# Feed-forward entry turned token-major, with modulation work redistributed between TensorE and VectorE

## The chip, the cores and the metric

The kernel runs on one core of one Trainium2 chip. The metric is the device time of one launch in microseconds (us); lower is better. The engines are named as the profile names them: PE (TensorE), DVE (VectorE), ACT (ScalarE), POOL (GpSimd) and SP (SyncE, which issues nearly all loads).

## The reference

The input is one sequence of 256 tokens with 1,024 features, all in float32. A first block (projections, an mLSTM mixer, an attention mixer, an output product, a gated unit with a norm) is followed by two layers of a second block. Cut to what matters here:

```python
c_act = silu(c)
for i in range(2):
    mod = (c_act @ mod_w[i] + mod_b[i]).reshape(B, 6, D)[:, :, None, :]
    hin = x * (1.0 + mod[:, 1]) + mod[:, 0]
    y = mla_mixer(hin, ...) if i == 0 else moba_mixer(hin, ...)
    x = layer_norm(ALPHA * x + mod[:, 2] * y, ln_g[i, 0], ln_b[i, 0])
    hin = x * (1.0 + mod[:, 4]) + mod[:, 3]
    u = hin @ ffn_w_in[i];  a, b = u[..., :D_FF], u[..., D_FF:]
    y = (gelu(causal_conv(a) + conv_b) * b) @ ffn_w_out[i]
    x = layer_norm(ALPHA * x + mod[:, 5] * y, ln_g[i, 1], ln_b[i, 1])
```

Each `mod[i][m]` is a vector of 1,024 numbers, and its weights are 4 MB, so the twelve vectors are 48 MB of loads and matrix-vector products that depend on `c` alone. They can be placed anywhere ahead of their use.

## The kernel before

**Products.** Every float32 weight tile of 128x1024 is split in two parts (`split`): ACT casts a high part `wh`, then DVE subtracts and writes a low part `wl`. Each of `wh` and `wl` has four buffers (NW), the raw loads have six of 1 MB (NR, tag "raw"). A product is three matmuls: high by high, high by low, low by high. In `mm3` the weight stands in the array and 256 tokens move (128x256); in `mm3t` a block of 128 tokens stands and 512 columns of weight move (128x512).

**Token-major stages.** `tokens` and `halves` compute a stage for token block 0 (tb 0) and then token block 1 (tb 1), both from the same split weights, in groups of weight rows k. Behind the last group of tb 0 stands `done(0)`, and behind that of tb 1 `done(1)`: `residual_moments` (DVE multiplies, adds, takes statistics), `rstd` (a power on POOL), then DVE scales the first half of x and ACT the second, and `feed` turns x by 128x128 transposes on PE (`ps_ln`) and writes its high part (`ln00h`, on ACT) and low part (`ln00l`, on DVE) for the next stage. Stages `mlay` and `mobay` (the mixers' output products) take tb 1 column by column in their last group (`by_column`), so that all four weight rows of it stay in use until the end of the stage.

**Norms.** `Norm(joint=True)` stands between a mixer and its feed-forward: it waits for both token blocks and then turns them together. Elsewhere the four pieces (first half of tb 0, then first half of tb 1, second half of tb 0, second half of tb 1) are turned one by one.

**Feed-forward entry.** The first 1,024 columns (`fi0`, `fi1`: four column blocks of the gated half and four of the other) are weight-stationary, because the norm gives x for both token blocks at once: 8 k x 8 column blocks x 3 matmuls of 128x256. Then come the other columns (`f`) and the output product (`fy`), interleaved.

**Modulation.** A vector is four units of 1 MB. A unit runs on PE (16 narrow matmuls, 8 in the order's rows, `ps_mod<-raw_mod,c`) or on DVE (two STT, short for SCALAR_TENSOR_TENSOR, of 128x1024 into `modacc`; the very first piece is an ACT multiply). `fin` closes a vector: if it has DVE parts, four more matmuls with ones sum them; then DVE adds the bias (`modr`) and PE turns the row (`modt`). `fill=N` of a stage puts N units on PE behind the last matmul of the stage, in the gap in which the norm is computed.

**What sets the order.** A scheduler with a timeline of its own orders each engine's instructions once, when the program is built; on the chip each engine takes them in that order. `issue_after` ties an instruction behind another for the scheduler, and buffers tie a split to the last use of the buffer's former content.

Of the kernel before, what the change touches and what calls it, by code (L numbers as in the profile page):

```python
# [46 lines left out]
class G:  # L47
# [182 lines left out]
    def halves(self, load, ks, x, acc, width, name, ends, done=None, fill=0, by_column=False):  # L230
# [275 lines left out]
def block1(g):  # L506
# [401 lines left out]
def gated(g, xt, hl, pw):  # L908
# [577 lines left out]
```

## Time and profile before

| | |
|---|---|
| median of 3 runs | 881.18 us (881.17 to 881.21) |
| the profiled execution | 881.07 us |
| its span, first to last instruction | 879.3 us |
| PE busy | 861.4 us, 98% |
| DVE, ACT, POOL busy | 645.9 us (73%), 482.7 us (55%), 52.9 us (6%) |
| granted clock of TensorE, mean | 0.997 |

The span is what the trace covers; about 1.8 us of the execution's time lie outside it. Times below are from the span's start. A matmul's shown duration is longer than its share of PE, since matmuls overlap: what one costs is the distance from its start to the next one's. The number in brackets behind a row is the time for which the engine sat idle before it, and what it waited for.

### The profile page before, as it was taken

To read this page: it belongs to the slowest core of one execution; us is meant where nothing else is said; L and a number is where in the kernel's file an instruction comes from. 1 tells how busy PE (TensorE), PEld (TensorE's weight loads), DVE (VectorE), ACT (ScalarE), POOL (GpSimd) and SP (SyncE) were. 2 spreads that over 40 slices of the span, in tenths; PEclk is the share of its full clock that TensorE was granted. 3 is DMA by queue.
4 is the path that set the end of the run, shared out by engine and by line. 5 is a ranking of instruction groups with operands and counts; after the bars stand their busy time and mean duration, and the time that the engine had idled before them with its cause. 6 is when DMAs were issued, how large, how long until landed. Compare 5 with 4: busy or idle time off the path is not lost. (4 is left out here: it accounts for less than half of the span.)

```text
span 879.3 us, 15479 instructions
## 1 busy us (share of the span) xinstructions
PE 861.4 (98%) x6119; PEld 776.4 (88%) x6119; DVE 645.9 (73%) x1201; ACT 482.7 (55%) x853; POOL 52.9 (6%) x81
## 2 busy tenths in 40 slices
PE   8999999999999999999999999999999999999996
PEld 7998779999888688799999899689997999999995
DVE  5798787768767585789888887575756676666676
ACT  6555666445567654476545556275553774454550
POOL 2003111000000230000000000000000000000003
PEclk9999999999999999999999999999999999999998
DMA  8955796854447972598898984598543965566311
GB/s 267 354 200 180 278 343 203 285 204 151 144 149 284 288 284 73 188 366 299 287 333 301 310 287 169 186 349 267 176 161 129 370 197 191 168 214 198 140 49 48
DMA packets 112766, 199.36 MB, mean 227 GB/s; under 512 B 8389, under 2 KB 76469, under 8 KB 112693
## 3 DMA queue, kind: packets, MB, share of 16 engines
q1 hardware_dynamic: 111892, 196.25, 65.6%
q0 software_dynamic: 496, 1.59, 0.5%
q8 instruction: 48, 0.79, 0.4%
q10 hardware_dynamic: 304, 0.53, 0.2%
q14 instruction: 26, 0.21, 0.1%
HBM read 197.28 MB, written 1.08 MB: 226 GB/s over the span
## 5 line engine op out<-in xcount | busy, mean ns | idle before, releaser
L187 PE MATMUL ps_f<-ln10h,wl_f 128*128 128x256 f32 x288 | 81.5, 283 | 0.0
L185 PE MATMUL ps_f<-ln10h,wh_f 128*128 128x256 f32 x288 | 81.5, 283 | 0.0
L186 PE MATMUL ps_f<-ln10l,wh_f 128*128 128x256 f32 x288 | 81.5, 283 | 0.0
L187 PE MATMUL ps_f<-ln00h,wl_f 128*128 128x256 f32 x288 | 81.5, 283 | 0.0
L186 PE MATMUL ps_f<-ln00l,wh_f 128*128 128x256 f32 x288 | 81.5, 283 | 0.0
L185 PE MATMUL ps_f<-ln00h,wh_f 128*128 128x256 f32 x288 | 81.4, 283 | 0.0
L172 ACT CAST wh_fo<-raw_fo 128x1024 fp32r<-128x1024 f32 x38 | 39.8, 1047 | 44.7 <-PE ps_f L186 43.5
L173 DVE TENSOR_TENSOR wl_fo<-raw_fo,wh_fo 128x1024 fp32r<-128x1024 f32 x38 | 46.5, 1223 | 20.8 <-ACT wh_fo L172 20.5
L172 ACT CAST wh_f<-raw_fa 128x1024 fp32r<-128x1024 f32 x36 | 37.5, 1048 | 39.3 <-PE ps_f L186 30.0
L974 DVE SCALAR_TENSOR_TENSOR modacc<-raw_mod,c,modacc 128x1024 f32<-128x1024 f32 x40 | 51.1, 1278 | 6.8 <-DMA raw_mod<-in_mod_w_dram 3.5
L173 DVE TENSOR_TENSOR wl_f<-raw_fb,wh_f 128x1024 fp32r<-128x1024 f32 x36 | 43.1, 1220 | 17.5 <-ACT wh_f L172 17.4
L186 PEld LDWEIGHTS ps_f<-ln00l,wh_f 128*128 128x128 f32 x288 | 55.2, 192 | 0.3
L185 PEld LDWEIGHTS ps_f<-ln00h,wh_f 128*128 128x128 f32 x288 | 55.2, 192 | 0.3
L173 DVE TENSOR_TENSOR wl_f<-raw_fa,wh_f 128x1024 fp32r<-128x1024 f32 x36 | 43.9, 1222 | 15.7 <-ACT wh_f L172 15.2
L187 PEld LDWEIGHTS ps_f<-ln00h,wl_f 128*128 128x128 f32 x288 | 55.2, 192 | 0.0
L187 PEld LDWEIGHTS ps_f<-ln10h,wl_f 128*128 128x128 f32 x288 | 55.1, 191 | 0.0
L186 PEld LDWEIGHTS ps_f<-ln10l,wh_f 128*128 128x128 f32 x288 | 55.1, 191 | 0.0
L185 PEld LDWEIGHTS ps_f<-ln10h,wh_f 128*128 128x128 f32 x288 | 55.1, 191 | 0.0
L172 ACT CAST wh_f<-raw_fb 128x1024 fp32r<-128x1024 f32 x36 | 36.6, 1047 | 29.0 <-PE ps_fy L194 22.2
L959 PE MATMUL ps_mod<-raw_mod,c 128*32 128x256 f32 x400 | 27.7, 383 | 0.9 <-DVE mod L989 0.9
L172 ACT CAST wh_fi<-raw_fi 128x1024 fp32r<-128x1024 f32 x16 | 16.9, 1074 | 14.9 <-PE ps_mlay L194 8.3
L959 PEld LDWEIGHTS ps_mod<-raw_mod,c 128*32 128x32 f32 x400 | 12.4, 109 | 11.8 <-issue 3.1
(839 smaller groups left out, 2848.1 us busy)
## 6 DMA issues: line engine op xcount, KB each, us to landing
raw_mod<-in_mod_w_dram SPq DMA_DIRECT2D x48, 1024.0 KB
raw_fo<-in_ffn_w_out_dram SPq DMA_DIRECT2D x22, 1024.0 KB
raw_fa<-in_ffn_w_in_dram SPq DMA_DIRECT2D x18, 1024.0 KB
raw_fb<-in_ffn_w_in_dram SPq DMA_DIRECT2D x18, 1024.0 KB
raw_fi<-in_ffn_w_in_dram SPq DMA_DIRECT2D x16, 512.0 KB
raw_wo<-in_w_out_dram SPq DMA_DIRECT2D x6, 1024.0 KB
raw_aqk<-in_w_in_dram SPq DMA_DIRECT2D x4, 1024.0 KB
raw_mqk<-in_w_in_dram SPq DMA_DIRECT2D x4, 1024.0 KB
```

Source lines behind the costliest of these rows:

```text
L172: self.nc.scalar.copy(hv, src)
L173: self.nc.vector.tensor_tensor(lv, src, hv.bitcast(F32), op=ALU.subtract)
L185: T.matmul(ps, wh, xh, start=start, stop=False, skip_group_check=chk)
L186: T.matmul(ps, wh, xl, start=False, stop=False, skip_group_check=chk)
L187: T.matmul(ps, wl, xh, start=False, stop=stop, skip_group_check=chk)
L959: T.matmul(st["ps"][32 * j:32 * j + 32, :], lhs, v[:, S * j:S * j + S], start=start, stop=stop, skip_group_check=True, tile_position=(0, 3 ...
L974: nc.vector.scalar_tensor_tensor(st["acc"], rv[:, e], c, st["acc"], op0=ALU.mult, op1=ALU.add)
```

## The change

The feed-forward entry becomes a token-major stage (`g.tokens` with `fload` and `fdone`): x stands, 512 weight columns move, 192 matmuls of 128x512 for each feed-forward stand where 384 of 128x256 stood. ACT copies the result to SBUF, and 16 transposes (`fit`) for each feed-forward turn it back for `gate` and `hidden`. The first two weight rows (`spare=2`) are split into raw buffers (`ws_fi`), ahead of the stage. The norm ahead of it is no longer joint; its four pieces are turned one by one, and the statistics of tb 1 are tied behind the scale of tb 0 (`g.marks`). In stages that aren't by column, the last three products (LATE) of tb 1 are tied behind the transposes of tb 0. The loads of `ukv` and `uq` stand ahead of `lat`'s modulation units, and the first two loads of `mobav` at the end of feed-forward 0.

The units on PE go from 25 to 10 and those on DVE from 23 to 38. The fills become: `pg` 2 to 0, `lat` 6 to 4, `mlay` 4 to 0, `fy0` 5 to 2, `mobay` 4 to 0. The vectors (0,4), (1,3) and (1,5) move to DVE in the stages `wo`, the moba heads and feed-forward 1, and in feed-forward 0 the slots for DVE units become two for each column block throughout. Ten vectors instead of six now have DVE parts, so 40 instead of 24 matmuls with ones close them.

```diff
@@ halves
-                ws[k] = self.split(load(k), f"{name}{k}", i >= NW)
+                ws[k] = self.split(load(k), f"{name}{k}", i < spare or i >= NW)
+        if pre is not None:
+            pre()
         self.fetch(fill)
...
-            with nullcontext() if ins is None or done is None else self.tc.issue_after(ins.ins):
-                for k, n, c in orders[tb]:
+            first = ins
+            for i, (k, n, c) in enumerate(orders[tb]):
+                with ExitStack() as ctx:
+                    if first is not None and done is not None:
+                        ctx.enter_context(self.tc.issue_after(first.ins))
+                        if self.turned is not None and not by_column and i >= len(orders[tb]) - LATE:
+                            ctx.enter_context(self.tc.issue_after(self.turned.ins))
@@ block1
-    g.tokens(a["w_out"][0], mix, [[8, 9], [10, 11], [0, 1], [2, 3], [4, 5, 6, 7]], wacc, hdone, "wo")
+    g.tokens(a["w_out"][0], mix, [[8, 9], [10, 11], [0, 1], [2, 3], [4, 5, 6, 7]], wacc, hdone, "wo",
+             each=lambda: g.bg(tensor=False))
@@ gated
-    g.tokens(a["w_ple_gate"][0], hl, [[0, 1], [2, 3, 4, 5, 6, 7]], gacc, done, "pg", fill=2)
+    g.tokens(a["w_ple_gate"][0], hl, [[0, 1], [2, 3, 4, 5, 6, 7]], gacc, done, "pg")
@@ Norm.emit
-        if self.joint:
-            todo = [((0, 1), lo + hi)] if tb else []
-        else:
-            todo = [((1,), lo), ((0,), hi), ((1,), hi)] if tb else [((0,), lo)]
+        todo = [((1,), lo), ((0,), hi), ((1,), hi)] if tb else [((0,), lo)]
@@ resid_ln
-        after = g.marks if tb and not out.joint else ()
+        after = g.marks if tb else ()
...
-        if out.joint == bool(tb):
+        if tb == 0:
             g.marks = [iv]
@@ mla
-    g.tokens(w, x, [[0, 1, 2, 3], [4, 5, 6, 7]], acc, done, "lat", width=cuts, fill=6)
+    first = []
+    g.tokens(w, x, [[0, 1, 2, 3], [4, 5, 6, 7]], acc, done, "lat", width=cuts, fill=4, pre=lambda: first.append(loads(0)))
...
-    g.tokens(a["mla_w_o_2"][0], o, [[0, 1], [2, 3], [4, 5, 6, 7]], part, lambda tb: done(tb, part), "mlay", fill=4, by_column=True)
+    g.tokens(a["mla_w_o_2"][0], o, [[0, 1], [2, 3], [4, 5, 6, 7]], part, lambda tb: done(tb, part), "mlay", by_column=True)
@@ moba
-        if (1, 3) not in g.have:
-            g.bg()
+        if st and (1, 3) not in g.have:
+            g.bg(0 if g.queue[0][1] is None else 1, tensor=False)
...
-    g.tokens(a["moba_w_o_2"][0], o, [[0, 1], [2, 3], [4, 5, 6, 7]], part, lambda tb: done(tb, part), "mobay", fill=4, by_column=True)
+    g.tokens(a["moba_w_o_2"][0], o, [[0, 1], [2, 3], [4, 5, 6, 7]], part, lambda tb: done(tb, part), "mobay", by_column=True)
@@ ffn
+    facc = g.pair(f"fi{i}")
+    ft = [g.b4(f"fi{i}t{tb}") for tb in range(2)]
...
+    def fdone(tb):
+        for n, c in enumerate(N512):
+            A.copy(ft[tb][:, c], facc(tb, n))
+
+    g.tokens(None, x, [[0, 1, 2, 3], [4, 5, 6, 7]], facc, fdone, f"fi{i}_", load=fload, spare=2)
     g.flush()
-    acc = [g.ps(f"fi{i}{n}", "A") for n in range(4)]
-    for k2 in range(0, KD, 2):
...
-                wh, wl = g.split(rv[:, j].rearrange("p e c -> p (e c)"), f"fi{i}_{k}")
-            for n in range(4):
-                for e in range(2):
-                    c = slice(512 * e + n * P, 512 * e + (n + 1) * P)
-                    g.mm3(acc[n][:, e * S:(e + 1) * S], wh[:, c], wl[:, c], *x[k], k == 0 and e == 0, k == KD - 1, chk=True)
...
     for n in range(4):
-        hidden(n, gate(n, acc[n][:, 0:S]), acc[n][:, S:2 * S])
+        ps = g.ps(f"fit{i}{n}", "A")
+        for e in range(2):
+            for tb in range(2):
+                c = 512 * e + n * P
+                T.transpose(ps[:, e * S + tb * P:e * S + (tb + 1) * P], ft[tb][:, c:c + P], g.ident)
+        hidden(n, gate(n, ps[:, 0:S]), ps[:, S:2 * S])
...
-        g.bg(2 if i == 0 and c < 16 else 1, tensor=False)
+        g.bg(1 if i else 2, tensor=False)
...
-    g.halves(load, list(range(last, NF)), hid, part, width, f"fo{i}_", ends, lambda tb: done(tb, part), 0 if i else 5, i == 1)
+    def pre():
+        if i == 0:
+            g.ahead = g.loader(a["moba_w_in_2"][0], 2048, D, "mobav")
+            g.ahead(0), g.ahead(2)
+
+    g.halves(load, list(range(last, NF)), hid, part, width, f"fo{i}_", ends, lambda tb: done(tb, part), 0 if i else 2, i == 1, pre)
```

**The entry of feed-forward 0, ACT.** `wh_fi_k` is the high part of weight row k (`ws_fi` where it is in a raw buffer), `x_72` and `x_73` are tb 0 and tb 1, `ln00h` the high part of the turned x. Behind the splits of `mlay` stood before:

```order
L172 CAST wh_fi_0_4447<-raw_fi_0_4444 128x1024
L1091 ACTIVATE x_72<-x_72,ln000nr,ln000ry 128x512
L1091 ACTIVATE x_73<-x_73,ln001nr,ln001ry 128x512
L348 ACTIVATE ln00h_4131<-ps_ln_4388,ln00ab,ln00as 128x256
L352 ACTIVATE ln00f_4393<-ps_ln_4388,ln00ab,ln00as 128x256
L348 ACTIVATE ln00h_4131<-ps_ln_4388,ln00ab,ln00as 128x256
L352 ACTIVATE ln00f_4397<-ps_ln_4388,ln00ab,ln00as 128x256
L172 CAST wh_fi_1_4475<-raw_fi_0_4444 128x1024
```

and now stands:

```order
L174 CAST wh_fi_2_4340<-raw_fi_2_4337 128x1024
L174 CAST wh_fi_3_4344<-raw_fi_2_4337 128x1024
L1104 ACTIVATE x_72<-x_72,ln000nr,ln000ry 128x512
L174 CAST wh_fi_4_4489<-raw_fi_4_4486 128x1024
L174 CAST wh_fi_5_4493<-raw_fi_4_4486 128x1024
L361 ACTIVATE ln00h_4112<-ps_ln_4269,ln00ab,ln00as 128x128
L365 ACTIVATE ln00f_4274<-ps_ln_4269,ln00ab,ln00as 128x128
L361 ACTIVATE ln00h_4112<-ps_ln_4269,ln00ab,ln00as 128x128 x2
```

Four casts of weight rows 2 to 5, two on either side of the scale of `x_72`, now stand ahead of the first piece of `ln00h`, where one cast stood. The order of feed-forward 1 reads the same with `fi1`, `ln10` and `mobay` for `fi0`, `ln00` and `mlay`.

**The same place on DVE.** `ln00nr`, `ln00t` and `ln00st` are steps of the norm, `wl_fi_k` the low part of weight row k, `ln00l` the low part of the turned x. From the scale of `x_72` on, before:

```order
L1089 SCALAR_TENSOR_TENSOR ln000nr<-ln000mv,ln000ry 128x1
L1090 TENSOR_SCALAR x_72<-x_72,ln000mv,ln000ry 128x512
L1061 SCALAR_TENSOR_TENSOR x_73<-x_73,ln001t_4375 128x256
L1062 BN_STATS ln001st<-x_73 128x6
L1063 BN_AGGR ln001mv<-ln001st 128x2
L1069 TENSOR_SCALAR ln001v<-ln001mv 128x1
L1089 SCALAR_TENSOR_TENSOR ln001nr<-ln001mv,ln001ry 128x1
L1090 TENSOR_SCALAR x_73<-x_73,ln001mv,ln001ry 128x512
L173 TENSOR_TENSOR wl_fi_0_4448<-raw_fi_0_4444,wh_fi_0_4447 128x1024
L984 SCALAR_TENSOR_TENSOR modr_4861<-ps_mod_4332,modb_4862 128x256
L353 TENSOR_TENSOR ln00l_4133<-ln00f_4393,ln00h_4131 128x256
```

and now:

```order
L1103 TENSOR_SCALAR x_72<-x_72,ln000mv,ln000ry 128x512
L175 TENSOR_TENSOR ws_fi_1_4334<-raw_fi_0_4328,ws_fi_1_4334 128x1024
L1073 TENSOR_TENSOR ln001t_4376<-ps_mlay_4145,row_ln00m 128x512
L1073 TENSOR_TENSOR ln001t_4380<-ps_mlay_4152,row_ln00m 128x256
L1073 TENSOR_TENSOR ln001t_4384<-ps_mlay_4159,row_ln00m 128x256
L175 TENSOR_TENSOR wl_fi_2_4341<-raw_fi_2_4337,wh_fi_2_4340 128x1024
L175 TENSOR_TENSOR wl_fi_3_4345<-raw_fi_2_4337,wh_fi_3_4344 128x1024
L1074 SCALAR_TENSOR_TENSOR x_73<-x_73,ln001t_4376 128x512
L1074 SCALAR_TENSOR_TENSOR x_73<-x_73,ln001t_4380 128x256
L1074 SCALAR_TENSOR_TENSOR x_73<-x_73,ln001t_4384 128x256
L175 TENSOR_TENSOR wl_fi_4_4490<-raw_fi_4_4486,wh_fi_4_4489 128x1024
L175 TENSOR_TENSOR wl_fi_5_4494<-raw_fi_4_4486,wh_fi_5_4493 128x1024
```

The first `ln00l` now stands behind one split into a raw buffer, the six steps of tb 1's statistics that carry `x_73`, and four more splits. On PE the units of `mod` that stood behind the last matmul of `mlay` are gone: four transposes of `x_72` and the product of `ws_fi_0` with `ln00h` follow directly.

**The stretch ahead of `wo` on DVE.** `mz`, `pw` and `wo` are weight products of the first block, `mzt`, `mnum` and `mixl` steps of its gate; `modacc` is vector (0,4). From the split of `wl_mz5` on, before:

```order
L173 TENSOR_TENSOR wl_mz_0_2520<-raw_mz_2480,wh_mz_0_2519 128x1024
L865 SCALAR_TENSOR_TENSOR mzt_2399<-mzt_2399,ps_mz_2370 128x256
L179 TENSOR_TENSOR mixl_2330<-mzt_2363,mixh_2328 128x256
L866 SCALAR_TENSOR_TENSOR mzt_2399<-to_2050,mzt_2399 128x256
L867 TENSOR_TENSOR mzt_2399<-mzt_2399,mnum_1825 128x256
L173 TENSOR_TENSOR wl_mz_0_2558<-raw_mz_2554,wh_mz_0_2557 128x1024
L865 SCALAR_TENSOR_TENSOR mzt_2437<-mzt_2437,ps_mz_2408 128x256
L179 TENSOR_TENSOR mixl_2330<-mzt_2399,mixh_2328 128x256
L866 SCALAR_TENSOR_TENSOR mzt_2437<-to_2108,mzt_2437 128x256
L867 TENSOR_TENSOR mzt_2437<-mzt_2437,mnum_1907 128x256
L173 TENSOR_TENSOR wl_mz_0_2594<-raw_mz_2554,wh_mz_0_2593 128x1024
```

and now:

```order
L175 TENSOR_TENSOR wl_mz_0_2520<-raw_mz_2480,wh_mz_0_2519 128x1024
L878 SCALAR_TENSOR_TENSOR mzt_2399<-mzt_2399,ps_mz_2370 128x256
L181 TENSOR_TENSOR mixl_2330<-mzt_2363,mixh_2328 128x256
L879 SCALAR_TENSOR_TENSOR mzt_2399<-to_2050,mzt_2399 128x256
L990 SCALAR_TENSOR_TENSOR modacc_2791<-raw_mod_2828,c,modacc_2791 128x1024
L880 TENSOR_TENSOR mzt_2399<-mzt_2399,mnum_1825 128x256
L175 TENSOR_TENSOR wl_mz_0_2558<-raw_mz_2554,wh_mz_0_2557 128x1024
L878 SCALAR_TENSOR_TENSOR mzt_2437<-mzt_2437,ps_mz_2408 128x256
L990 SCALAR_TENSOR_TENSOR modacc_2791<-raw_mod_2828,c,modacc_2791 128x1024
L181 TENSOR_TENSOR mixl_2330<-mzt_2399,mixh_2328 128x256
L175 TENSOR_TENSOR wl_mz_0_2594<-raw_mz_2554,wh_mz_0_2593 128x1024
L879 SCALAR_TENSOR_TENSOR mzt_2437<-to_2108,mzt_2437 128x256
```

Two of the seven STT of the vector stand in these rows; four more stand between here and the split of `wl_wo_10`, and one stands two splits earlier.

## Rows read from the trace of the kernel before

**Rows 1.** The page, part 1: busy time of each engine.

```profile
PE 861.4 (98%) x6119; PEld 776.4 (88%) x6119; DVE 645.9 (73%) x1201; ACT 482.7 (55%) x853; POOL 52.9 (6%) x81
```

**Rows 2.** The page, part 5: one STT of a modulation unit.

```profile
L974 DVE SCALAR_TENSOR_TENSOR modacc<-raw_mod,c,modacc 128x1024 f32<-128x1024 f32 x40 | 51.1, 1278 | 6.8 <-DMA raw_mod<-in_mod_w_dram 3.5
```

**Rows 3.** Windows: busy us of PE, PEld, DVE, ACT, POOL; PEclk; DMA.

```profile
185.00:225.00 40.00, 40.00 (x270) 36.92 (x269) 32.80 (x64) 24.11 (x41) 0.00 (x0) 1.00 0.47 156
...
396.00:560.00 164.00, 164.00 (x1145) 151.85 (x1145) 135.39 (x187) 84.84 (x123) 0.55 (x1) 1.00 0.78 272
```

**Rows 4.** Timeline of PE: `mlay`, modulation, `ln00`, `fi0`, first `f` product.

```profile
360.08 0.39 PE L192 MATMUL ps_mlay<-wh_mlay,mlaoh 128*128 128x512 f32 x1
360.31 0.39 PE L193 MATMUL ps_mlay<-wl_mlay,mlaoh 128*128 128x512 f32 x1
...
365.76 3.66 PE L959 MATMUL ps_mod<-raw_mod,c 128*32 128x256 f32 x64
369.35 0.55 PE L343 MATMUL ps_ln<-ident,x 128*128 128x128 f32 x3
...
371.44 0.74 PE L185 MATMUL ps_fi<-ln00h,wh_fi 128*128 128x256 f32 x4
...
395.45 0.28 PE L185 MATMUL ps_f<-ln00h,wh_f 128*128 128x256 f32 x1
```

**Rows 5.** Timeline of ACT in the same place.

```profile
364.79 1.05 ACT L172 CAST wh_fi<-raw_fi 128x1024 fp32r<-128x1024 f32 x1 [8.31 <-PE ps_mlay L194]
367.21 0.81 ACT L1091 ACTIVATE x<-x,ln000nr,ln000ry 128x512 f32<-128x512 f32 x1 [1.36 <-DVE ln000nr L1089]
```

**Rows 6.** Timeline of DVE and POOL in the same place.

```profile
354.81 3.49 DVE L173 TENSOR_TENSOR wl_mlay<-raw_mlay,wh_mlay 128x1024 fp32r<-128x1024 f32 x3
...
359.83 1.29 DVE L1060 TENSOR_TENSOR ln000t<-ps_mlay,row_ln00m 128x512 f32<-128x512 f32 x2 [1.53 <-PE ps_mlay L194]
...
362.24 1.28 DVE L1062 BATCH_NORM_STATS2 ln000st<-x 128x6 f32<-128x512 f32 x2
...
365.60 0.67 POOL L303 TENSOR_TENSOR ln000ry<-ln000v,mhalf 128x1 f32<-128x1 f32 x1 [33.33 <-DVE ln000v L1069]
```

**Rows 7.** Timeline of ACT and DVE behind `fy0`: feed pieces of 128x128.

```profile
564.12 0.46 ACT L348 ACTIVATE ln01h<-ps_ln,ln01ab,ln01as 128x128 fp32r<-128x128 f32 x1 [4.17 <-PE ps_ln L343]
564.48 0.45 ACT L352 ACTIVATE ln01f<-ps_ln,ln01ab,ln01as 128x128 f32<-128x128 f32 x1
...
566.25 0.41 DVE L350 TENSOR_SCALAR ln01f<-ps_ln,ln01as,ln01ab 128x128 f32<-128x128 f32 x1
```

**Rows 8.** Timeline of PE: `mobay` to first `f` product of FFN 1.

```profile
676.74 3.66 PE L959 MATMUL ps_mod<-raw_mod,c 128*32 128x256 f32 x64
...
706.47 0.28 PE L185 MATMUL ps_f<-ln10h,wh_f 128*128 128x256 f32 x1
```

**Rows 9.** Timeline of DVE and PE: `fy0` to `mobaq`.

```profile
559.02 0.54 DVE L1090 TENSOR_SCALAR x<-x,ln010mv,ln010ry 128x512 f32<-128x512 f32 x1
...
562.44 1.06 PE L959 MATMUL ps_mod<-raw_mod,c 128*32 128x256 f32 x12
...
594.32 0.28 PE L185 MATMUL ps_mobaq<-ln01h,wh_mobaq 128*128 128x256 f32 x1
```

**Rows 10.** Timeline of PE: `pg` to `kn`.

```profile
270.01 0.63 PE L959 MATMUL ps_mod<-raw_mod,c 128*32 128x256 f32 x6
...
302.45 0.39 PE L185 MATMUL ps_kn<-ckh,wh_ukv 128*128 128x256 f32 x1
```

**Rows 11.** Timeline of DVE and PE: first split of `wo`, and its use.

```profile
205.94 1.23 DVE L173 TENSOR_TENSOR wl_wo<-raw_wo,wh_wo 128x1024 fp32r<-128x1024 f32 x1 [0.19 <-ACT wh_wo L172]
...
208.78 0.40 PE L193 MATMUL ps_wo<-wl_wo,ha0h 128*128 128x512 f32 x1
```

**Rows 12.** Timeline of PE in FFN 0: the products that end one modulation vector.

```profile
429.48 0.64 PE L959 MATMUL ps_mod<-modacc,ones 128*32 128x256 f32 x8
```

**Rows 13.** Windows at the end of the program (columns as in rows 3).

```profile
876.00:879.30 3.30, 0.00 (x0) 0.00 (x0) 0.11 (x1) 0.00 (x0) 0.00 (x0) 0.50 0.45 159
```

More of the change, by code (lines that the diff above doesn't have):

```diff
@@ L33 @@
 WARM = 15
+LATE = 3
 NW, NR = 4, 6
@@ L65, in __init__ @@
         self.queue, self.early, self.have = [], [], set()
+        self.ahead = None
     def ps(self, name, tag):
@@ L261, in halves, with tokens @@
             self.pending = lambda: done(1)
-    def tokens(self, w, x, groups, acc, done, name, c0=0, width=None, fill=0, by_column=False):
+    def tokens(self, w, x, groups, acc, done, name, c0=0, width=None, fill=0, by_column=False, pre=None, load=None, spare=0, each=None):
         width = (N512, TAIL) if by_column else (width or N512,) * 2
-        load = self.loader(w, c0, width[0][-1].stop, name)
+        load = load or self.loader(w, c0, width[0][-1].stop, name)
         for ks in groups:
-            end = (done, fill, by_column) if ks is groups[-1] else ()
+            end = (done, fill, by_column, pre) if ks is groups[-1] else (None, 0, False, None, spare)
             self.halves(load, ks, x, acc, width, name, (groups[0][0], groups[-1][-1]), *end)
+            spare = 0
+            if each is not None and ks is not groups[-1]:
+                each()
     def loader(self, w, c0, n, name):
@@ L1083, in done @@
         z, h = prev[tb], f"{name}{tb}"
-        cols = TAIL if tb and out.joint else N512
-        after = g.marks if tb and not out.joint else ()
+        cols = TAIL if tb and j == 0 else N512
+        after = g.marks if tb else ()
         mean, var = residual_moments(g, h, z, lambda n: acc(tb, n), cols, scale, after)
@@ L1197, in done, with loads @@
         A.copy(kx[:, t], p2[:, 0:P])
+    def loads(hf):
+        rv = g.wload(a["mla_w_ukv_2"][0], 0, 2, 1024 * hf, 1024, f"ukv{hf}")
+        raw = g.raw(f"uq{hf}")[:, 0:2 * 768].rearrange("p (k c) -> p k c", k=2)
+        for k in range(2):
+            src = a["mla_w_uq_2"][0][k * P:(k + 1) * P, 768 * hf:768 * hf + 768].rearrange("p (h c) -> p h c", h=4)
+            nc.sync.dma_start(raw[:, k, 0:512].rearrange("p (h c) -> p h c", h=4), src[:, :, 0:P])
+            nc.sync.dma_start(raw[:, k, 512:768].rearrange("p (h c) -> p h c", h=4), src[:, :, P:192])
+        return rv, raw
     acc = lambda tb, n: lacc(tb, n, (256, 320)[n])
[L1200 removed]
+    first = []
+    g.tokens(w, x, [[0, 1, 2, 3], [4, 5, 6, 7]], acc, done, "lat", width=cuts, fill=4, pre=lambda: first.append(loads(0)))
     g.flush()
@@ L1224, in units @@
     def units(hf):
-        rv = g.wload(a["mla_w_ukv_2"][0], 0, 2, 1024 * hf, 1024, f"ukv{hf}")
-        raw = g.raw(f"uq{hf}")[:, 0:2 * 768].rearrange("p (k c) -> p k c", k=2)
-        for k in range(2):
-            src = a["mla_w_uq_2"][0][k * P:(k + 1) * P, 768 * hf:768 * hf + 768].rearrange("p (h c) -> p h c", h=4)
-            nc.sync.dma_start(raw[:, k, 0:512].rearrange("p (h c) -> p h c", h=4), src[:, :, 0:P])
-            nc.sync.dma_start(raw[:, k, 512:768].rearrange("p (h c) -> p h c", h=4), src[:, :, P:192])
+        rv, raw = first.pop() if first else loads(hf)
         with ExitStack() as ctx:
@@ L1304, in moba @@
     vacc = g.pair("mobav")
+    load = g.ahead or g.loader(w, 2048, D, "mobav")
     vt = [g.b4(f"mobav{tb}") for tb in range(2)]
```

46 lines of the change are left out of this document (22 added, 24 removed).

## The prediction

> **What bounds the kernel now.** I read the page's busy times first: PE is busy for 861.4 of 879.3 us, 98% [rows 1]. So the kernel is a single line of PE work, and the time can change in two ways only: PE gets less to do, or it waits more. Next come the windows, which tell where another engine is near its own limit and could make PE wait: DVE is busy for 32.80 of 40 us ahead of and in `wo`, and for 135.39 of 164 us in feed-forward 0 [rows 3]. Last come the timelines at each place where a norm stands between two stages, since there PE has nothing of its own to do and lives on modulation units: behind `mlay` the 64 instructions of four units fill the time from 365.76 to 369.35 us, that is 0.90 us for a unit, and the first product of `fi0` follows at 371.44 us [rows 4]. The question is what PE does in these gaps when the units are gone.
>
> **The plain sum of PE work.** Start-to-start prices: 0.23 us for a 128x512 product (360.08 to 360.31) and 0.12 us for a 128x256 one: `fi0` with its 192 products takes 24.0 us, from 371.44 to 395.45, waits included [rows 4]. The 15 units that leave PE are worth 15 x 0.90 = 13.5 us. The 384 entry products of 0.12 us become 192 of 0.227 us: -2.5 us. The 32 transposes back cost about 0.11 us each, as the twelve of the norm between 369.35 and 371.44 do without their wait: +3.5 us. Four more vectors have to be closed by ones-products, which take 0.64 us a time where one can see them in feed-forward 0 [rows 12]: +2.6 us. If PE never waited for more than before, the sum would be -13.5 - 2.5 + 3.5 + 2.6 = -9.9 us. The units do not vanish, though: they become 26 more STT of 1.28 us on DVE [rows 2]. So I work through the gaps one by one.
>
> **The two feed-forward entries.** This is the step that decides. Let E = 365.76 us be the end of `mlay`. Tb 0 is finished early enough: its chain starts on DVE at 359.83, each pair of steps takes 1.2 us, and the statistics are through by 363.5 [rows 6]; with about 0.4 us for the two small steps, 0.67 us on POOL and 0.7 us for `nr` and the scale, the first half of x is scaled at 365.4. PE can therefore turn it at E, in four transposes, to 366.2.
> Then the built order bites. ACT: the first cast of a weight row of the entry waits for `mlay` and started at 364.79 before, since only then a buffer comes free [rows 5]; nothing in the change frees it earlier. In the new order two casts of 1.05 us, the scale of x (0.81 us, of which 0.75 until the next can start) and two more casts all stand ahead of the first `ln00h`: 364.79 + 4 x 1.05 + 0.75 = 369.7, and the piece itself takes 0.36 us until the next one starts [rows 7], so PE gets it at 370.0. DVE: from 365.4 on, one split (three took 3.49 us, so 1.16 each [rows 6]), three products of the statistics (0.65 + 0.35 + 0.35), two splits, three additions (1.35), two splits: 365.4 + 5 x 1.16 + 2 x 1.35 = 373.9, and `ln00l` is there at 374.1. PE waits from 366.2 to 370.0, does the four products that need only the high part, to 370.9, and waits again to 374.1. The other 20 products of tb 0 take 4.54 us and wait some 0.4 us for the next low parts, which now share DVE with tb 1's statistics: 379.0. By then tb 1 is scaled. Twelve transposes (1.3) to 380.3, 72 products (16.3) to 396.6, 16 transposes back (1.75): the columns `f` start, in effect, at 398.4, where they started at 395.45 [rows 4]. So a saving of four units (3.6 us) turns into a **loss of 2.9 us**. At the entry of feed-forward 1 the same instructions stand in the same order, and the stretch before is as long (676.74 to 706.47, 29.73 us, against 29.69 [rows 8]): another **2.9 us**. Bounds for each: at best PE waits only for ACT and DVE to do the feed of tb 0 at once, which would give -2 us; at worst the waits are 1 us longer: +4 us.
>
> A pause of PE can cost twice. At the end of the program, with no matmul left, the granted clock is 0.50 in the last 3.3 us [rows 13], which is the lower of the two levels, 1.2 of 2.4 GHz; everywhere else in the rows it is 1.00. The two pauses of an entry, 3.8 and 3.2 us with 0.9 us of products between, are longer than any in the trace before the end. If the clock fell there and the 24 products of tb 0 ran at half speed, an entry would lose 5.4 us more. The Trainium skill states the rule in "TensorE: Matmul & The Clock Gate", section "HAM oscillation — how this bites in real kernels": leave no long idle gaps on PE, or it is throttled again and starts cold. By that rule the sum below would rise by up to 10.8 us; the trace agrees only in so far as the clock does fall when PE has run out of work. I keep it as a rival.
>
> **The gap behind `fy0`.** Here x of tb 0 is scaled at 559.6 and `fy0` ends at 562.44 [rows 9], so the new early transposes and the first loads of `mobav` work: one split now precedes the scale (1.2 us, so 560.8), the transposes stand ahead of the last nine products, and the first `ln01h` is ready when the two remaining units end (564.3). Ones-products (0.65), 24 products of tb 0 (5.45) to 570.4; tb 1's statistics, between the feeds on DVE, are through at about 571.8; twelve transposes (1.3), 72 products (16.3), some 0.7 us of small waits: `mobaq` starts at 590.1 where it started at 594.32. **Gain 4.2 us** (2 to 4.5).
>
> **Between `pg` and `kn`.** Before, 270.01 to 302.45 [rows 10]. Four units go (3.6 us); of the first two about 1.2 us comes back as a wait for tb 1's scale, since the 24 products of `lat` for tb 0 last 3.1 us only; one `modt` moves away and the casts of `ukv` come earlier. **Gain 2.9 us** (1 to 3.6).
>
> **The stretch ahead of `wo`.** Vector (0,4) puts seven STT here. DVE is idle for 7.2 of 40 us [rows 3] and gets 7 x 1.2 = 8.4 us, so it must fall behind by 1.2 us at least. `wl_wo8` was written from 205.94 to 207.17 and first used at 208.78 [rows 11]: 1.6 us of slack. Going along the order with 1.2 us for each STT, I find that split at 208.3 to 209.5 and the next one about 1.1 us late too. **Loss 1.5 us** (0 to 4: the unit's loads wait for buffers that late splits release).
>
> **Closing the vectors.** The four more groups of ones-products stand inside dense PE work: **loss 2.6 us** (2 to 3.5).
>
> **At nothing.** The other STT: in feed-forward 0 five more, 6 us on a DVE that is busy for 135 of 164 us [rows 3], so 86% instead of 82%; without that cover each would cost 1.2 us. Those among the moba heads and in feed-forward 1 fall where DVE is less busy still. The copies of `fi` on ACT stand beside products.
>
> **Sum.** 2.9 + 2.9 - 4.2 - 2.9 + 1.5 + 2.6 = +2.8 us on the profiled execution of 881.07 us, which lies 0.11 us under the median: 884.0 us.
>
> **The rivals.**
> 1. *The entries gain.* Place: ACT and DVE at E. If the four casts could run before `mlay` ends, or the feed got ahead of them, each entry would give -2 instead of +2.9 us, and the sum becomes 2.8 - 9.8 = -7.0: 874 us. It decides when `ln00l` is there by about 371 instead of 374. For it: PE has x at 366.2. Against it: the order of both engines, and the buffers released at 364.79 only.
> 2. *PE work alone counts.* No gap opens anywhere: -9.9, 871 us. For it: PE at 98%. The Trainium skill's "Perfetto Trace Analysis", section "Identifying the Most-Contended Engine", says to optimise the engine with the highest occupancy first, which the change does. Against it: the gaps above.
> 3. *The clock falls* in the entries: +5 to +10 us, 889 to 895. For it: two pauses of over 3 us almost next to each other. Against it: 0.9 us of products stand between, and no such pause stands in the trace before the end.
> 4. *The change does nothing measurable*: the entries lose a little less and `wo` nothing, and it all cancels. Within 0.2% (1.8 us), which is about what a measurement of this kernel can tell from no change.
>
> **How the numbers follow.** Entries lose, sum as above, 880.5 to 888: 0.57, of which 0.10 falls within 0.2%. Rival 1: 0.22. Rival 2: 0.07. Rival 3: 0.10. The rest, 0.04, ends within 0.2% by other ways. So faster 0.29, same 0.14, slower 0.57. The predicted time is that of the likeliest case, 884.0 us; its own range is 880.5 to 888. For 8 in 10 the range has to take in rival 1 and the near end of rival 3: 873 to 889.
>
> **What would show it.** Right: in the timeline of PE behind `mlay` and `mobay`, two waits of 3 to 4 us, the first ended by ACT's `ln00h`, the second by DVE's `ln00l`; `f` begins 32 to 33 us after the end of `mlay` instead of 29.7; `mobaq` about 27.7 us after the end of `fy0` instead of 31.9; DVE over 36 of 40 us ahead of `wo`. Wrong: `ln00l` within 5 us of the end of `mlay`, or a granted clock under 1.00 there. The prediction fails most easily on the entries, which carry 5.8 us of loss where 7 us were saved.

## The result and the profile after

| | before | after |
|---|---|---|
| median | 881.17 us | 902.81 us (901.79, 902.81 and 903.94) |
| ratio | | 1.0245, 95% interval 1.0228 to 1.0262 |
| the profiled execution, and its span | 881.07, 879.3 us | 901.79, 900.0 us |
| granted clock of TensorE, mean | 0.997 | 0.984 |

The change costs 21.6 us; forecast were 2.8. One execution of the changed kernel (1059.25 us, clock 0.748) and one of `e_old_warm` (3984.96 us) were disturbed, and the medians and ratios leave them out.

The page of after, part 1, which answers to [rows 1]:

```profile
PE 861.7 (96%) x5751; PEld 767.8 (85%) x5751; DVE 680.7 (76%) x1259; ACT 493.7 (55%) x881; POOL 52.2 (6%) x81
```

PE is busy for as long as before, though 15 units left it, and idle for 38.3 us instead of 17.9. Windows of after (columns as in [rows 3]):

```profile
185.00:225.00 40.00, 38.29 (x264) 34.28 (x263) 35.25 (x62) 21.08 (x36) 0.00 (x0) 1.00 0.69 242
...
372.00:380.00 8.00, 6.17 (x15) 4.39 (x14) 6.57 (x18) 2.01 (x5) 0.60 (x1) 0.50 0.86 274
380.00:384.00 4.00, 4.00 (x24) 3.42 (x24) 1.44 (x2) 2.15 (x4) 0.00 (x0) 0.95 0.01 4
...
396.00:560.00 164.00, 161.75 (x1138) 149.03 (x1139) 138.03 (x187) 90.59 (x130) 0.00 (x0) 0.99 0.79 275
...
408.00:416.00 8.00, 7.94 (x67) 7.73 (x65) 8.00 (x13) 5.08 (x9) 0.00 (x0) 1.00 0.67 238
416.00:420.00 4.00, 1.82 (x4) 1.49 (x5) 4.00 (x8) 3.83 (x10) 0.00 (x0) 0.74 0.82 284
420.00:424.00 4.00, 4.00 (x21) 2.60 (x20) 4.00 (x10) 0.45 (x2) 0.00 (x0) 0.83 0.64 208
...
691.00:701.00 10.00, 7.27 (x16) 5.28 (x17) 8.06 (x19) 3.45 (x9) 0.55 (x1) 0.50 0.87 280
...
730.00:738.00 8.00, 5.72 (x43) 5.34 (x43) 8.00 (x16) 5.87 (x11) 0.00 (x0) 1.00 0.72 229
```

Two things stand out: a granted clock of 0.50 in both entries (372 to 380 and 691 to 701 us), and a DVE without a free moment from 408 to 424 us and from 730 to 738 us, where PE waits. The timeline of PE in after, which answers to [rows 4, 9, 10]:

```profile
273.79 0.28 PE L194 MATMUL ps_lat<-wh_lat,fnh 128*128 128x256 f32 x1
...
303.64 0.28 PE L187 MATMUL ps_kn<-ckh,wh_ukv 128*128 128x256 f32 x1
...
367.28 0.60 PE L356 MATMUL ps_ln<-ident,x 128*128 128x128 f32 x4
371.41 0.80 PE L194 MATMUL ps_fi<-ws_fi,ln00h 128*128 128x512 f32 x1 [3.52 <-ACT ln00h L361]
372.00 0.63 PE L195 MATMUL ps_fi<-ws_fi,ln00h 128*128 128x512 f32 x1
372.43 0.63 PE L194 MATMUL ps_fi<-ws_fi,ln00h 128*128 128x512 f32 x1
...
375.31 1.22 PE L196 MATMUL ps_fi<-ws_fi,ln00l 128*128 128x512 f32 x2 [1.83 <-DVE ln00l L366]
...
382.37 1.47 PE L356 MATMUL ps_ln<-ident,x 128*128 128x128 f32 x12
...
390.83 1.21 PE L196 MATMUL ps_fi<-wh_fi,ln00l 128*128 128x512 f32 x4 [1.06 <-DVE ln00l L366]
...
402.65 0.36 PE L187 MATMUL ps_f<-ln00h,wh_f 128*128 128x256 f32 x1
...
405.73 1.69 PE L1417 MATMUL ps_fit<-ident,fi0t 128*128 128x128 f32 x14
...
418.18 0.80 PE L194 MATMUL ps_fy<-wh_fo,fh0h 128*128 128x512 f32 x1 [2.25 <-ACT fh0h L180]
...
577.55 1.93 PE L975 MATMUL ps_mod<-raw_mod,c 128*32 128x256 f32 x32
...
603.71 0.28 PE L187 MATMUL ps_mobaq<-ln01h,wh_mobaq 128*128 128x256 f32 x1
...
691.69 0.79 PE L194 MATMUL ps_fi<-ws_fi,ln10h 128*128 128x512 f32 x1 [3.52 <-ACT ln10h L361]
...
695.80 1.22 PE L196 MATMUL ps_fi<-ws_fi,ln10l 128*128 128x512 f32 x2 [2.04 <-DVE ln10l L366]
...
736.57 0.50 PE L194 MATMUL ps_fy<-wh_fo,fh1h 128*128 128x512 f32 x1 [2.28 <-ACT fh1h L180]
...
739.52 0.50 PE L196 MATMUL ps_fy<-wh_fo,fh1l 128*128 128x512 f32 x1 [0.83 <-DVE fh1l L181]
```

Both pauses are there in each entry, ended by the engines that were forecast. But the products between and behind them start 0.43 us apart (372.00, 372.43) where a product of this size takes 0.23 us in [rows 4]: half the pace. And two waits follow that were not forecast, at 390.83 and 418.18 us; in feed-forward 1 there are two as well, at 736.57 and 739.52 us. The timeline of DVE shows what DVE did ahead of them (`wl_wo` answers to [rows 11]; `fs` are steps of the gate of the first hidden columns):

```profile
208.38 1.22 DVE L175 TENSOR_TENSOR wl_wo<-raw_wo,wh_wo 128x1024 fp32r<-128x1024 f32 x1
...
372.70 2.35 DVE L175 TENSOR_TENSOR wl_fi<-raw_fi,wh_fi 128x1024 fp32r<-128x1024 f32 x2
374.97 0.28 DVE L366 TENSOR_TENSOR ln00l<-ln00f,ln00h 128x128 fp32r<-128x128 f32 x1
...
389.29 1.28 DVE L990 SCALAR_TENSOR_TENSOR modacc<-raw_mod,c,modacc 128x1024 f32<-128x1024 f32 x1 [2.94 <-DMA raw_mod<-in_mod_w_dram]
390.49 0.49 DVE L366 TENSOR_TENSOR ln00l<-ln00f,ln00h 128x128 fp32r<-128x128 f32 x2
...
414.96 1.27 DVE L990 SCALAR_TENSOR_TENSOR modacc<-raw_mod,c,modacc 128x1024 f32<-128x1024 f32 x1
416.15 1.21 DVE L175 TENSOR_TENSOR wl_fo<-raw_fo,wh_fo 128x1024 fp32r<-128x1024 f32 x1
417.29 1.40 DVE L1387 TENSOR_TENSOR fs<-fs,ps_fit 128x256 f32<-128x256 f32 x4
```

At 389.29 us DVE has waited 2.94 us for the load of a modulation unit, and the `ln00l` that PE needs stands behind it. At 414.96 us an STT and a split stand ahead of the step that `fh0h` waits for. ACT begins the gate of the first hidden columns late, too. Before, the timeline of ACT has it at

```profile
393.60 1.17 ACT L1360 ACTIVATE fs<-ps_fi,cols 128x256 f32<-128x256 f32 x2
```

and in after at

```profile
406.64 1.93 ACT L1380 ACTIVATE fs<-ps_fit,cols 128x256 f32<-128x256 f32 x4
```

Where the time went, from the starts of the same products in the two traces (the terms of the forecast beside them; the closing of vectors, +2.6, was not put at a place):

| stretch | forecast | measured |
|---|---|---|
| start to end of `mlay` | +1.5 - 2.9 | +1.6 |
| end of `mlay` to first `fy0` | +2.9 | +9.6 |
| rest of feed-forward 0 | 0 | +3.9 |
| `fy0` to `mobaq` | -4.2 | -5.7 |
| `mobaq` to end of `mobay` | 0 | +1.5 |
| end of `mobay` to first `fy1` | +2.9 | +7.7 |
| rest of feed-forward 1 | 0 | +2.1 |

### The profile page after: what moved, and what is told of

The parts are those of the page before. It is cut to its first block, busy times and chain, and to the rows that moved or that the text cites. A ratio compares the mean times of both kernels' runs of the same rounds, so it can differ in the third digit from the quotient of the medians.

```text
span 900.0 us, 14848 instructions
## 1 busy us (share of the span) xinstructions
PE 861.7 (96%) x5751; PEld 767.8 (85%) x5751; DVE 680.7 (76%) x1259; ACT 493.7 (55%) x881; POOL 52.2 (6%) x81
## 5 line engine op out<-in xcount | busy, mean ns | idle before, releaser
L990 DVE SCALAR_TENSOR_TENSOR modacc<-raw_mod,c,modacc 128x1024 f32<-128x1024 f32 x66 | 84.4, 1279 | 30.2 <-DMA raw_mod<-in_mod_w_dram 18.2
L174 ACT CAST wh_f<-raw_fb 128x1024 fp32r<-128x1024 f32 x36 | 36.7, 1047 | 26.2 <-PE ps_fy L196 19.9
L1383 ACT ACTIVATE fs<-fs 128x256 f32<-128x256 f32 x44 | 17.8, 413 | 8.9 <-DVE fs L1382 8.7
L174 ACT CAST wh_fi<-raw_fi 128x1024 fp32r<-128x1024 f32 x12 | 12.1, 1044 | 17.4 <-PE ps_mlay L196 8.3
L1380 ACT ACTIVATE fs<-ps_f,cols 128x256 f32<-128x256 f32 x36 | 19.9, 554 | 0.0
```

Source lines behind the costliest of these rows:

```text
L174: self.nc.scalar.copy(hv, src)
L990: nc.vector.scalar_tensor_tensor(st["acc"], rv[:, e], c, st["acc"], op0=ALU.mult, op1=ALU.add)
L1380: A.activation(s, pa, AF.Identity, bias=cb[:, n:n + 1], scale=cw[:, 2, n:n + 1])
L1383: A.activation(s, s, AF.Gelu_apprx_tanh)
```

## The experiments

All times are medians, ratios are to the kernel before. "Fills" are the four units behind each of `mlay` and `mobay` that the change removed. A new edit makes the scheduler move other instructions as well: in e_warm and e_old_warm, for example, some splits and STT stand in another order on DVE from the second half of the entry on.

**Idle transposes in the first pause** (e_warm). After, with 34 transposes that nothing reads behind the first four of each entry.

```diff
+    wps = g.ps(f"warm{i}", "V")
+    with g.tc.issue_after(g.tail.ins):
+        for _ in range(34):
+            T.transpose(wps[:, 0:P], g.ident, g.ident)
```

> The changed kernel with 34 idle 128x128 transposes (about 3.7 us at full clock) behind the first four transposes of each feed-forward entry, which compute nothing that is used; no wait of the real work is taken away. If the lost time is mostly the halved clock: the granted clock stays at 1.00 in at least the first pause, the entry products cost 0.23 us instead of 0.43 us, and the time falls by 5 to 9 us to 893 to 897. If it is the waits and the order themselves, the clock matters little: within 2 us of the changed kernel's 902.8.

899.38 us, 1.0205 (1.0188 to 1.0223): 3.4 us less than after, between its two forecasts. The first pause is filled, the second stays, as the timeline of PE shows,

```profile
375.62 1.22 PE L196 MATMUL ps_fi<-ws_fi,ln00l 128*128 128x512 f32 x2 [2.71 <-DVE ln00l L367]
```

and the granted clock still falls: 0.87 in 360 to 380 us (after: 0.75) and 0.91 in 680 to 700 us (after: 0.78). So this run doesn't give the price of the clock.

**Feed first** (e_feed). The splits of weight rows 2 to 5 are tied behind the feed of tb 0.

```diff
+    lead = {2: g.fed[1], 3: g.fed[3], 4: g.fed[3], 5: g.fed[3]}
+    g.tokens(..., spare=2, lead=lead)
```

> The changed kernel with the splits of entry rows 2 to 5 tied behind the feed pieces of token block 0, nothing else. If the order of splits and feed makes the two pauses (and these the fall of the clock): first product within 2 us of the end of the mixer's output product, no second pause over 1 us, clock 1.00, and the time falls by 9 to 14 us to 889 to 894. If the entry's late result and the later stages cost the time whatever happens in the gap: it falls by less than 4 us.

897.80 us, 1.019 (1.0175 to 1.0206). No pause in the entries is longer than 1.8 us now, and the clock is 1.00 in 360 to 380 and 680 to 700 us. Yet only 5.0 us return, between the two forecasts, because the waits for the low parts and the hidden columns stay, as the timeline of PE in this kernel shows:

```profile
416.10 0.50 PE L194 MATMUL ps_fy<-wh_fo,fh0h 128*128 128x512 f32 x1 [2.00 <-ACT fh0h L180]
...
420.60 0.47 PE L194 MATMUL ps_fy<-wh_fo,fh0h 128*128 128x512 f32 x1 [0.87 <-DVE fs L1389]
```

A full clock in the entries was not enough.

**Fills back** (e_fill), and **the entry of before without fills** (e_oldentry): the change's two main parts, each undone alone.

```diff
-... part, lambda tb: done(tb, part), "mlay", by_column=True)
+... part, lambda tb: done(tb, part), "mlay", fill=4, by_column=True)
```

(and the same for `mobay`), and for e_oldentry the `ffn` entry, `joint` and `resid_ln` as they stood before. In e_fill vector (1,5), now on PE, is also summed in the buffer that it had before.

> The changed kernel with the four modulation units back on TensorE behind each mixer's output product (eight units, so vectors (0,5) and (1,5) on TensorE). If the pauses and the clock are the loss: units fill the first pause, the clock stays at 1.00, VectorE has 14 fewer long instructions in the feed-forwards, and the time falls by 10 to 16 us to 887 to 893. If the token-major entry costs the time itself: it falls by less than 5 us, since 7.2 us of unit work comes back onto TensorE.

> The changed kernel with the old feed-forward entry (weight-stationary, both token blocks turned together) and everything else as changed, so also without units behind the mixers' output products. If the new entry is the loss: 875 to 882, since the gap behind the first feed-forward and the stretch ahead of the latent stage gave 8 us and the ones-products and the stretch ahead of the output product of block 1 took 5 us. If the missing units are the loss (pause, then a halved clock): TensorE stands idle for 4 us at each entry, the clock falls there, and the time is 885 to 895.

e_fill: 884.12 us, 1.0029 (1.0019 to 1.0039). e_oldentry: 884.67 us, 1.0038 (1.0023 to 1.0053). Each alone takes away most of the 21.6 us: 18.7 us by the one, 18.1 by the other. e_fill is below its forecast, e_oldentry between its two. The loss is made by the two together.

**Both undone** (e_old_fill), and **the new entry alone in the kernel before** (e_newentry; the diff is the `ffn` entry of the change, with `spare`, `load` and the norms that go with it). Its counterpart **fills and feed first** (e_fill_feed) joins the edits of e_fill and e_feed.

> The changed kernel with the old entry and with four units back behind each mixer's output product; what is left of the change is vector (0,4) in the stretch ahead of the output product of block 1, the empty gap behind the gated stage, the earlier loads, the late products, vector (1,3) on VectorE and two units instead of five behind feed-forward 0. If these parts are worth what the timelines showed (1.2 to 1.9 us lost before the first mixer's end, 5.7 us won behind feed-forward 0, about 1 us for each further closing of a vector): 876 to 880, faster than before. If the won time is given back later: 881 or more.

> The kernel before with the token-major entry and the norm half by half ahead of it, and no other part of the change: all 25 units stay on TensorE, four of them in each gap. If the entry costs little while its gap is filled and VectorE is not loaded: 881 to 885, for 1 us more TensorE work and 1 to 2 us of waits at each entry. If the entry is slow in itself (copies, transposes back, late hidden columns): 888 or more.

> The changed kernel with four units back behind each mixer's output product and with the splits of entry rows 2 to 5 tied behind the feed of token block 0. Against the kernel with the units alone (882.6 to 885.4): if the remaining pauses of 1.6 us and 2.5 us in its entries come from splits ahead of the feed, it is 2 to 4 us faster, 879 to 882. If they come from VectorE being full whatever the order: within 1 us of it.

e_old_fill: 878.85 us, 0.9967 (0.9956 to 0.9978), faster than both kernels by little, as forecast. e_newentry: 886.29 us, 1.0053 (1.0037 to 1.0069), between its two forecasts. e_fill_feed: 883.03 us, 1.0013 (1.0003 to 1.0024), 1.1 us from e_fill, so the order of the splits matters little once the units are back. So the rest of the change is worth about -2.5 us, and the token-major entry costs about 5 us even with its gaps filled:

| | entry of before | token-major entry |
|---|---|---|
| with fills | 878.85 | 884.12 |
| without fills | 884.67 | 902.81 |

Without the entry the missing fills cost 5.8 us, with it 18.7: 12.9 us belong to neither alone.

**Units out of the heads** (e_late). No DVE unit in the first two column blocks of each feed-forward, three for each block later in feed-forward 0.

```diff
-        g.bg(1 if i else 2, tensor=False)
+        g.bg(0 if c < 8 else 1 if i else 3, tensor=False)
```

> The changed kernel with no modulation unit on VectorE in the first two column blocks of each feed-forward (three units a block later in feed-forward 0), nothing else. If the output product's wait on the first hidden columns comes from the long modulation instructions that share VectorE with the gate: the waits of 2.4 us (feed-forward 0) and 3.5 us (feed-forward 1) ahead of and in the first output products fall under 0.7 us, the wait for a low part inside the entry (1.2 us) goes, and the time falls by 5 to 9 us to 894 to 898. If that wait comes from the transposes back alone: less than 2 us.

900.85 us, 1.0209 (1.0192 to 1.0226): 2 us less than after. The wait ahead of `fy0` is gone, but the gain is lost again: two of the waits that came instead, late in feed-forward 0, in the timeline of PE:

```profile
528.62 0.38 PE L187 MATMUL ps_f<-ln00h,wh_f 128*128 128x256 f32 x1 [1.31 <-ACT wh_f L174]
...
563.51 0.80 PE L195 MATMUL ps_fy<-wl_fo,fo_16h 128*128 128x512 f32 x1 [2.08 <-DVE wl_fo L175]
```

So the units cost time in both places that were tried in this stage, and the next runs change their number. This run also speaks against a rival, that the STT cost time only because DVE stands still for their loads: it waits 18.2 us in all for such loads in after and 2.4 us here, and the time falls by 2 us only.

**Fewer units on DVE** (e_drop), and **that with feed first** (e_feed_drop). The DVE additions of vectors (0,5) and (1,5) are left out, so these two vectors are incomplete; loads and products stay.

```diff
-                    else:
+                    elif m != 5:
                         nc.vector.scalar_tensor_tensor(st["acc"], rv[:, e], c, st["acc"], op0=ALU.mult, op1=ALU.add)
```

> The changed kernel with the six VectorE additions of two modulation vectors, (0,5) and (1,5), left out in the column heads and entries (their values stay incomplete; all loads and products remain). Theory A (VectorE's added scalar-tensor-tensor units delay the low parts and the late hidden columns): the first fy product no longer waits, and the time falls by 8 to 10 us to about 893. Theory B (order of the splits and the clock alone): it falls by 2 us or less, 899 to 903.

> The same two vectors' additions left out, and the splits of later pieces tied behind the feed of the first. Theory A+B (split order and VectorE's load are together all of the entries' loss): 884 to 888. If a third cause is at work (the transposes moved back, the products' own pace), it stays above 890.

The expectation counts six additions; the edit takes out 14 STT, seven for each vector. e_drop: 891.89 us, 1.0125 (1.0107 to 1.0143). e_feed_drop: 884.62 us, 1.0044 (1.0027 to 1.0061). The first is a little beyond the forecast of theory A, the second within its own. In e_drop, 52 STT of units instead of 66, the first `fy0` product follows the last `f` product at once, though the pauses of the entries are those of after (3.52 and 1.82 us in feed-forward 0) and the clock is low there too (0.84 and 0.74 in its windows 360 to 380 and 680 to 700 us, 0.75 and 0.78 in after); the timeline of PE:

```profile
417.25 0.28 PE L189 MATMUL ps_f<-ln00h,wl_f 128*128 128x256 f32 x1
417.37 0.40 PE L194 MATMUL ps_fy<-wh_fo,fh0h 128*128 128x512 f32 x1
```

In e_feed_drop the pauses are short too, and the products run at 0.23 us, in the timeline of PE:

```profile
368.08 0.50 PE L194 MATMUL ps_fi<-ws_fi,ln00h 128*128 128x512 f32 x1 [0.55 <-ACT ln00h L363]
368.42 0.39 PE L195 MATMUL ps_fi<-ws_fi,ln00h 128*128 128x512 f32 x1
368.65 0.39 PE L194 MATMUL ps_fi<-ws_fi,ln00h 128*128 128x512 f32 x1
```

| | splits first | feed first |
|---|---|---|
| 66 STT | 902.81 | 897.80 |
| 52 STT | 891.89 | 884.62 |

10.9 us for 14 STT, 7.3 us more for the order with the clock: 18.2 of the 21.6 us. e_fill has 52 STT as well, with eight more units on PE, which by [rows 4] are 7.2 us of work; it takes as long as e_feed_drop. So the work that the change took from PE in these gaps had cost next to nothing.

**The clock alone** (e_old_warm). e_oldentry with 34 idle transposes behind `mlay` and `mobay`.

```diff
+        if by_column and name != "fo1_":
+            wps = self.ps(f"warm{name}", "V")
+            with self.tc.issue_after(ins.ins):
+                for _ in range(34):
+                    self.nc.tensor.transpose(wps[:, 0:P], self.ident, self.ident)
```

> The entry of before in the changed kernel's other parts, without the four fill units behind mlay and mobay, and 34 idle transposes (nothing reads them) in their place. Theory 'clock': the 6 us between this kernel without and with the fill units are the price of TensorE's clock, so 877.5 to 879.5 us. Theory 'load': they are the price of the units that VectorE then carries, so 882 us or more.

880.76 us, 0.9999 (0.9989 to 1.0009), between the two forecasts: of the 5.8 us that part e_oldentry from e_old_fill the idle transposes give back 3.9, and 1.9 stay. The timelines of PE behind `mlay`, first of e_oldentry:

```profile
369.04 0.63 PE L356 MATMUL ps_ln<-ident,x 128*128 128x128 f32 x3 [1.94 <-DVE x L1106]
371.49 2.18 PE L356 MATMUL ps_ln<-ident,x 128*128 128x128 f32 x9 [1.82 <-DVE x L1106]
373.32 1.20 PE L187 MATMUL ps_fi<-ln00h,wh_fi 128*128 128x256 f32 x4
...
374.53 0.41 PE L189 MATMUL ps_fi<-ln00h,wl_fi 128*128 128x256 f32 x1
374.75 0.41 PE L187 MATMUL ps_fi<-ln00h,wh_fi 128*128 128x256 f32 x1
```

and of e_old_warm:

```profile
366.87 3.87 PE L274 MATMUL ps_warmmlay<-ident 128*128 128x128 f32 x34
...
371.43 1.20 PE L361 MATMUL ps_ln<-ident,x 128*128 128x128 f32 x9 [0.36 <-DVE x L1111]
372.63 0.74 PE L187 MATMUL ps_fi<-ln00h,wh_fi 128*128 128x256 f32 x4
...
373.77 0.28 PE L189 MATMUL ps_fi<-ln00h,wl_fi 128*128 128x256 f32 x1
373.89 0.28 PE L187 MATMUL ps_fi<-ln00h,wh_fi 128*128 128x256 f32 x1
```

The last nine transposes begin at about the same moment in both (371.49 and 371.43 us), but a 128x256 product costs 0.22 us in the one and 0.12 in the other, at a granted clock of 0.83 and of 1.00 in 360 to 380 us. Up to these rows nothing differs but the idle transposes and the clock. From the last product of the mixer to the first of `fy0` and `fy1` the two kernels are 1.75 and 1.54 us apart: 3.3 of the 3.9 us. The rest lies later in feed-forward 0, where the order differs too.

**The `wo` stretch relieved** (e_best3). e_old_fill without units tied to the splits of `wo`, with two fills behind `pg`, and one vector's rest on DVE in the mla heads.

```diff
-    g.tokens(..., wacc, hdone, "wo",
-             each=lambda: g.bg(tensor=False))
+    g.tokens(..., wacc, hdone, "wo")
...
-... gacc, done, "pg")
+... gacc, done, "pg", fill=2)
...
-            g.bg(0 if g.queue[0][1] is None else 1)
+            g.bg(0 if g.queue[0][1] is None else 1, tensor=False)
```

> The entry of before, the fill units back at mlay and mobay, no units tied to each split in the wo stretch, two fill units back ahead of pg, one vector's rest on VectorE in the mla heads. If the 2.2 to 2.7 us by which pg starts late come from VectorE's units in the wo stretch, 875 to 877.5; if not, 878 to 880.

880.08 us, 0.999 (0.9981 to 1.0), 1.2 us above e_old_fill and at the upper end of the second forecast. `pg` starts at 247.49 us, as before (247.54), instead of 249.76 in e_old_fill, so the loss ahead of `pg` does come from the units in `wo`. The time does not follow, since DVE is late one stage further on, in the timeline of PE:

```profile
294.46 0.44 PE L1002 MATMUL ps_modt<-ident,modr 128*128 128x128 f32 x2 [3.09 <-DVE modr L999]
298.23 1.34 PE L1206 MATMUL ps_ltT<-ident,lt 128*128 128x128 f32 x4 [3.33 <-DVE lt L1197]
```

## Why the prediction was wrong in size

The direction was right, and so was the cause that was given for it, the pauses of the entries. Two steps failed: the pace of PE behind the pauses, and the cover of the STT.

**Right: what ends the pauses, and when.** PE was to get `ln00h` 4.2 us and `ln00l` 8.3 us after the end of `mlay`; it got them at 371.41 and 375.31, 4.1 and 8.0 us after 367.28, ended by ACT and DVE as said. Rival 1 is excluded. The second pause is 1.83 us and not 3.2, mostly because the four products ahead of it ran at half pace.

**Wrong: "the other 20 products of tb 0 take 4.54 us".** From 375.31 to 382.37 they took 7.06 us, most of it at the lower level of the clock (0.50 until 380 us, 1.2 GHz). At 0.23 us each they would have taken 4.6 us, so the clock cost 2.5 us in this entry, and 2.6 us in feed-forward 1 (695.80 to 703.02 us), where the window has the same 0.50. The four products between the pauses were slow as well, but that only shortened the wait for `ln00l`. This is rival 3, which I had priced at 5.4 us an entry, given a chance of 0.10 and left out of the sum; a granted clock under 1.00 in the entries stood among the signs of being wrong. The argument against it, that 0.9 us of products stand between the pauses, did not hold. The columns `f` begin 35.4 us behind the end of `mlay` (402.65 - 367.28), not 32 to 33. (In each feed-forward 96 products of 128x512 stand where 192 of 128x256 stood; 192 and 384 are the two together.) The Trainium skill ("TensorE: Matmul & The Clock Gate", section "HAM oscillation — how this bites in real kernels") warns of just such idle gaps; the trace agrees, with the 0.50 above. By that rule alone the sum would have been 2.8 + 10.8 = 13.6 us, and 894.7 us, so it too leaves 7 us unexplained.

**Wrong: "At nothing: the other STT".** The cover was read from a mean over 164 us. That mean came out as forecast (138.03 of 164 us by the window of after, 84% against 86%), but in the head of the stage DVE has no free moment (408 to 424 us), and what PE waits for stands in DVE's order behind STT and splits. Before, the gate's first step on ACT stood at 393.60 us, ahead of the first `f` product at 395.45; now the columns are copied and turned back first (405.73 us), and that step stands at 406.64, 4 us behind the first `f` product. So what stands between the gate's steps on DVE is on the path: 2.25 us of waits in feed-forward 0, 2.28 and 0.83 in feed-forward 1, behind STT and splits together. The 1.06 us in the entry are the STT that waited for its load; in feed-forward 1 an STT at 726.89 us, ahead of the gate's steps, held DVE for 2.76 us in the same way. e_drop puts 10.9 us on the 14 STT. Its trace shows where: against after, the way from the end of `mlay` to the first `fy0` is 3.4 us shorter, the rest of feed-forward 0 3.1, the way from the end of `mobay` to the first `fy1` 2.3 and the rest of feed-forward 1 1.2. From `mobaq` to the end of `mobay` it is as long as after, so the +1.5 us there do not come from these STT.

**Undersized: the stretch ahead of `wo`.** `wl_wo8` was forecast at 208.3 to 209.5 us and stands at 208.38 to 209.60. But `pg` starts 3.4 us late, not 1.5 and a group of closing matmuls: PE waits 1.7 us (44.29 of 46 us busy from 205 to 251 us), and the rest, in which the closing of (0,4) lies, was not taken apart. DVE was to be over 36 of 40 us busy and was at 35.25.

**Right: `pg` to `kn`.** From the end of `pg` to `kn` it takes 303.64 - 273.79 = 29.9 us against 32.4 in [rows 10]: 2.6 us gained, forecast 2.9.

**Right, and better: behind `fy0`.** 603.71 - 577.55 = 26.2 us against 31.9 in [rows 9]: 5.7 us gained, forecast 4.2. In e_old_fill this stretch is as short, and it is the only one in which that kernel is clearly ahead of the kernel before. Three units fewer on PE, at 0.90 us by [rows 4], make 2.7 us of it; the rest is left to the early transposes and loads, which no run undid alone.

**How it adds up.** From the last product of the mixer to the first product of `fy0` or `fy1`, in us, by the starts in the traces:

| | to `fy0` | to `fy1` |
|---|---|---|
| before | 41.41 | 41.46 |
| new entry alone (e_newentry) | 43.97 | 43.88 |
| after | 51.02 | 49.13 |
| after, 14 STT fewer (e_drop) | 47.59 | 46.87 |
| after, 14 STT fewer and feed first (e_feed_drop) | 43.41 | 42.82 |
| after with the old entry (e_oldentry) | 43.15 | 42.99 |
| the same with idle transposes (e_old_warm) | 41.40 | 41.45 |

The missing fills act in two ways. PE has nothing to do in the pauses, so the clock falls there; and the same units, now on DVE, delay the low parts and the hidden columns behind the pauses, though not the pauses themselves, which e_drop leaves as they are. The second is dear only with the new entry. With the old one, idle transposes alone bring both stretches back to those of before, with all 66 STT still on DVE; with the new one, the gate's steps stand behind the first `f` products, and DVE's order decides when `fy` can begin. The first costs with both: 3.3 us came back with the old entry, and the slow products alone are 5.1 us with the new one, where the pauses are longer too. That is why undoing either the fills or the entry brought back 18 to 19 us, and why I could not have got 21.6 us as a sum of terms taken one at a time.

What stays open: the price of the clock in the changed kernel by itself. e_warm raised it only in part, and e_feed changed the order with it; 2.5 us an entry is read from the pace of the products, without what the lower clock behind 418.18 us (0.74 and 0.83) cost.

## What to carry to other kernels

Here work in a gap of the bounding engine was free until the gap closed; before such work is moved away, ask what fills the gap then, and whether the engine that takes the work is the one that ends the gap. Read an engine's cover from the stretch in which the chain runs through it, not from the mean of the stage. Where a sum has a rival that halves the clock, price the pauses with it.

## What the runs showed of the hardware

Pauses of nearly one length did not have one result. Behind the wait of 2.25 us at 418.18 us the granted clock was 0.74 and then 0.83; behind the wait of 2.28 us that ends at 736.57 us in feed-forward 1 it stayed at 1.00 (the window 730 to 738 us above, and on to 752 us). And two waits of 1.94 and 1.82 us with three transposes between them, in e_oldentry, brought it down to 0.83 in 360 to 380 us. Even one and the same pause differed: after and e_drop have the same order on PE, DVE, ACT and POOL up to 380 us, and in both PE waits 2.26 us for DVE behind `pg`, ahead of the transposes at 279.39 and 280.66 us; in 280 to 284 us the granted clock was 1.00 in the execution of after and 0.66 in that of e_drop. From these rows I could not say beforehand which pause costs twice.
